# Splitting the last weight tile of a chunk's second product on VectorE, and one buffer for both parts of a split tile

## The chip, the cores and the metric

The kernel runs on one core of one Trainium2 chip. The metric is the device time of one launch in microseconds. Before the change three runs gave 2721.76, 2721.63 and 2718.28 us (median 2721.63 us). The execution that the profiler recorded took 2719.21 us, and its span is 2717.2 us.

## The reference

The reference is a trunk of two encoder layers, applied to 512 prompt tokens and 256 sample tokens with the same weights. The change lies in the loading of weights, and it alters arithmetic in the second half of a layer only: the feed-forward part with hidden width 4096 and model width 1024.

```python
def encoder_layer(x, l, ...):
...
    x = x + merged @ w_out
    h2 = rmsnorm(x, norm2_g)
    return x + jnp.square(jax.nn.relu(h2 @ w_ff1)) @ w_ff2
```

## The kernel before

All 768 tokens stand side by side on the free axis, and the model dimension lies on the 128 partitions, in 8 tiles. TensorE works on float32 data that is split in two: `hi` is the value rounded to the matmul's input type, `lo` is the rest. Each product of two split operands is three matmuls, `hi*hi`, `hi*lo` and `lo*hi`, which add up in PSUM (lines 1100 to 1103 for the second product). So every weight tile of 128x1024 is loaded, then split into `whi` and `wlo`, and TensorE reads both.

The feed-forward part goes through the hidden width in 8 chunks of 512. A chunk has a first product (`wf1`, lines 1017 to 1048) and a second product (`wf2`, lines 1081 to 1111). Both use a scheme of seven block products in place of eight. Its seven weight operands are made from four loaded blocks `a1`, `b1`, `b2`, `a2`: four are sums or differences (`P1` to `P4`, made on VectorE in line 250), three are the loaded blocks `a1`, `a2` and `b2` themselves. The order in which the first product takes them is `FW` (a1, P1, P2, a2, P3, P4, b2). The second product takes its seven products in the order `FP2` = (1, 2, 7, 6, 5, 3, 4), whose weight operands by `FW2` are a1, a2, P3, P2, P1, P4, b2. So **q=4, with weight operand b2, is the last product of a chunk**, and the first product of the next chunk begins with its own a1. Each q is 24 matmuls of 128x384. The last chunk of layer 1 uses the plain form (`wf2s`) for its second product. There are thus 15 chunks with seven-fold second products (7 in layer 1, 8 in layer 2) and 16 seven-fold first products.

The two kinds of weight operand are split in two ways (function `prefetch`). A sum or difference is split by `split`: ScalarE copies it to `whi` (line 210) and VectorE subtracts (`wlo = src - whi`, line 213). A loaded block (a1, a2, b2) is split by ScalarE and a DMA: ScalarE writes `whi` (line 294), then writes `-whi` into `wlo` (line 295), and a DMA that POOL issues adds the same block to `wlo` from DRAM (line 296):

```python
S.activation(hi, raw, AF.Copy)
S.activation(lo, raw, AF.Copy, scale=-1.0)
G.dma_start(out=lo, in_=acc, accum_op=ALU.add)
```

There are 93 of these accumulating DMAs. The second element that `ff_operand` returns is the DRAM address of the block, or None for a sum, and it decides which way `prefetch` takes.

Weights are prepared 8 plan entries ahead of their use (`AHEAD`), in a ring of four `whi` and four `wlo` buffers (`WB` = 4). A buffer comes free when TensorE has run the last matmul that reads it. The order of the instructions on each engine is settled at build time by a list scheduler with priorities; the additions of the second product from PSUM (line 1108, shown under its helper's line 1069) and the splits of the hidden activations (`h_split`, line 1065, shown under lines 210 and 213) have a raised priority. The activations' split for q=4 is `o2[4]`, made in line 1091.

Of the kernel before, what the change touches and what calls it, by code (L numbers as in the profile page):

```python
# [10 lines left out]
F32R = mybir.dt.float32r  # L11
# [5 lines left out]
P = 128  # L17
# [47 lines left out]
WB = 4  # L65
# [18 lines left out]
def trunk_kernel(ctx: ExitStack, tc: tile.TileContext, xT, wqk, wv, wx, wy, wg0, wg1, wa, wr, wo, wf1, wf2,  # L84
# [5 lines left out]
    wp = ctx.enter_context(tc.tile_pool(name="wp", bufs=1))  # L90
# [112 lines left out]
    def nm(s):  # L203
        uid[0] += 1
        return f"{s}_{uid[0]}"

    def split(hi, lo, src, eng="act"):

        if eng == "act":
            S.activation(hi, src, AF.Copy)  # L210
        else:
            V.tensor_copy(out=hi, in_=src)
        V.tensor_tensor(out=lo, in0=src, in1=hi.bitcast(F32), op=ALU.subtract)  # L213
# [29 lines left out]
    fw, fpool = {}, [None]  # L243

    def ff_operand(w, l, c, x):

        ep_, sub = fpool[0], w == "wf2"

        def two(out, u, v, op):
            V.tensor_tensor(out=fw[out], in0=fw[u], in1=fw[v], op=op)  # L250

        if x == "a1":
            for i, y in enumerate(("a1", "b1", "b2", "a2")):
                if i < 2:
                    fw[y] = ep_.tile([P, 1024], F32, tag="rw", name=nm("rw"), bufs=4)
                else:
                    fw[y] = wp.tile([P, 1024], F32, tag="raw", name=nm("raw"), bufs=3)
                fw["d" + y] = WT[w][l][c][i]
                nc.sync.dma_start(out=fw[y], in_=fw["d" + y])
            fw["P1"] = fw["P2"] = None  # L260
        if x in ("P1", "P2", "P3") and fw["P1"] is None:
            fw["P1"] = ep_.tile([P, 1024], F32, tag="ws", name=nm("ws"), bufs=2)
            two("P1", "b1", "b2", ALU.add)
        if x == "P2":
            fw[x] = ep_.tile([P, 1024], F32, tag="ws", name=nm("ws"), bufs=2)
            two(x, "P1", "a1", ALU.subtract if sub else ALU.add)
        elif x == "P3":
            fw[x] = fw["b1"]
            two(x, "a1", "b1", ALU.subtract if sub else ALU.add)
        elif x == "P4":  # L270
            fw[x] = fw["P2"]
            two(x, "a2", "P2", ALU.subtract if sub else ALU.add)
        return fw[x], fw.get("d" + x)

    def prefetch(upto):
        while len(ready) < min(upto, len(plan)):
            k = plan[len(ready)]
            acc = None
            if k[0] in ("wf1", "wf2"):
                (raw, acc), n = ff_operand(*k), 1024  # L280
            else:
                src = WT[k[0]]
                for x in k[1:]:
                    src = src[x]
                n = src.shape[1]
                raw = wp.tile([P, n], F32, tag="raw", name=nm("raw"), bufs=3)
                nc.sync.dma_start(out=raw, in_=src)
            hi = wp.tile([P, n], F32R, tag="whi", name=nm("whi"), bufs=WB)
            lo = wp.tile([P, n], F32R, tag="wlo", name=nm("wlo"), bufs=WB)
            if acc is None:  # L290
                split(hi, lo, raw)
            else:
# [4 lines that stand above are left out]
            ready.append((hi, lo))  # L297

    def wload(*key):
        i = pos[0]  # L300
        pos[0] += 1
        assert plan[i] == key, (plan[i], key)
        prefetch(i + 1 + AHEAD)
        r, ready[i] = ready[i], None
        return r
# [101 lines left out]
    def slot(tag, dt=F32):  # L407

        if (tag, dt) in spare:
            return spare.pop((tag, dt))  # L410
        t_ = slots(tag, dt)
        spare[tag, dt] = t_[:, 1]
        return t_[:, 0]
# [7 lines left out]
    def norm1(l, xt, alloc):  # L421

        nh = [slot(gh, F32R) for k in range(KT)]
        nl = [slot(gl, F32R) for k in range(KT)]
        ss, st_ = [], []

        def sums():
            if not st_:
                st_.append(slots(gx, F32R))
            return st_[0]  # L430

        for g in range(2):
            if g:
                prefetch(4)
            ss.append(squares(xt, g, alloc, sums, lambda k: prep(xt, vt[l][:, V_N1:V_N1 + KT], nh, nl, g, k)))
        return nh, nl, ss
# [6 lines left out]
    for k in range(KT):  # L443
        if k % 4 == 0:
            prefetch(1 + k // 4)
        nc.sync.dma_start(out=xt[k][:, 0:TA], in_=xT[k][:, 0:TA])
# [7 lines left out]
    for l in range(DEPTH):  # L454
# [292 lines left out]
        def chain():  # L747
            for kind, i in FILL:
                yield from (vproj(i, rtok) if kind == "wv" else proj(i, rtok) if kind == "wqk" else gate0(rb))

        n, it = 0, chain()
# [13 lines left out]
        for k in range(KT):  # L765
            af = ep.tile([P, T], F32, tag="af", name=nm("af"), bufs=4)
            G.dma_start(out=af, in_=ats[k])
            hi = ep.tile([P, T], F32R, tag="e", name=nm("ath"))
            lo = ep.tile([P, T], F32R, tag="e", name=nm("atl"))
# [6 lines left out]
        for j in range(KT):  # L776
# [3 lines left out]
            for g in range(2):  # L780
                off, n = GROUPS[g]
# [118 lines left out]
        def eslot(dt=F32):  # L900
            return ep.tile([P, T], dt, tag="e", name=nm("e"), bufs=16)

        def rslot(dt=F32):
            return recp.tile([P, T], dt, tag="r", name=nm("r"))

        rch, rcl = [], []
        for k in range(KT):
            hi, lo = eslot(F32R), eslot(F32R)
# [7 lines left out]
        for j in range(KT):  # L916
# [5 lines left out]
            for g in range(2):  # L922
                off, n = GROUPS[g]
# [4 lines left out]
            hi, lo = (rslot(F32R) if j < 4 else slot(gl, F32R) for i in range(2))  # L928
# [49 lines left out]
        for j in range(KT):  # L978
            w1 = wload("wo", l, j)
            for g in range(2):  # L980
                off, n = GROUPS[g]
# [21 lines left out]
        for c in range(NC_):  # L1003
# [13 lines left out]
            for i, (p, q) in enumerate(FP):  # L1017
                x, b = {1: ("a1", 2), 5: ("P1", 3), 6: ("P2", 2), 2: ("a2", 1), 7: ("P3", 2), 4: ("b2", 2), 3: ("P4", 3)}[q]
                if x not in ws:
                    ws[x] = [a.rearrange("p (h k c) -> p h k c", h=2, c=P) for a in wload("wf1", l, c, x)]  # L1020
                hi, lo = (a[:, p] for a in ws[x])
# [50 lines left out]
            if str2:  # L1072
# [8 lines left out]
                for q in FP2:  # L1081
# [10 lines left out]
                    hi, lo = (a.rearrange("p (r k c) -> p r k c", r=4, c=P) for a in wload("wf2", l, c, FW2[q]))  # L1092
# [19 lines left out]
            else:  # L1112
# [3 lines left out]
                for s in range(4):  # L1116
                    hi, lo = (a.rearrange("p (j k c) -> p j k c", j=2, c=P) for a in wload("wf2s", l, s))
# [99 lines left out]
```

## Time and profile before

| | us | share of the span |
|---|---|---|
| median of three runs | 2721.63 | |
| the profiled execution, own time | 2719.21 | |
| its span | 2717.2 | 100% |
| TensorE (PE) busy | 2617.4 | 96% |
| VectorE (DVE) busy | 1979.9 | 73% |
| ScalarE (ACT) busy | 1575.4 | 58% |
| POOL busy | 176.3 | 6% |

The seven-fold chunks of layer 1 run from about 870 to 1300 us, those of layer 2 from about 2223 us to the end. Matmuls overlap in the trace: one of 128x384 is shown as 0.33 us long, and the next starts 0.17 us after it. An idle time is counted from the shown end of the matmul before. In the rows, names that end in `wlo` and `whi` are weight parts, `raw`, `rw` and `ws` the unsplit weights, `sX`, `sY`, `sZ` and `e` activations, `d` a PSUM tile. The clock column of a stretch is the granted clock of TensorE as a share of 2.4 GHz; 0.50 is 1.2 GHz.

### The profile page before, as it was taken

How to read it: one execution, taken by the hardware profiler on the slowest of the kernel's cores; microseconds unless marked ns; L12 is line 12 of the kernel's file. 1: busy time of each engine (PE TensorE's matmuls, PEld its weight loads, DVE VectorE, ACT ScalarE, POOL GpSimd, SP SyncE). 2: the span in 40 equal slices, each digit the busy share in tenths (PEclk: the TensorE clock that was granted, in tenths of full speed). 3: DMA queues.
4: the chain of work that ended last, by engine and by line, in shares of the span. 5: the costliest groups of instructions: out<-in, count | busy, mean ns of one | idle time of the engine just before them, and what ended most of it. 6: DMA issues, size and time to landing. Idle time of an engine off the chain costs nothing. (4 is left out here: it accounts for less than half of the span.)

```text
span 2717.2 us, 40429 instructions
## 1 busy us (share of the span) xinstructions
PE 2617.4 (96%) x16096; PEld 2450.1 (90%) x16096; DVE 1979.9 (73%) x3243; ACT 1575.4 (58%) x2570; POOL 176.3 (6%) x227
## 2 busy tenths in 40 slices
PE   8999999999999999999999999999999999999999
PEld 8999888888889999998999998888888899999898
DVE  8878873797658777777678788637984587777776
ACT  7778871568336445444467878716683364544444
POOL 0000000000120000000100000000001100000000
PEclk9999999999999999999999999999999999999999
DMA  4111123112433444444421111231224334454543
GB/s 138 53 49 59 40 89 125 59 63 74 149 99 86 109 109 116 110 116 101 120 72 51 49 55 52 97 103 57 74 63 166 92 76 116 110 117 111 121 109 93
DMA packets 70876, 248.07 MB, mean 91 GB/s; under 512 B 8992, under 2 KB 12448, under 8 KB 70688
## 3 DMA queue, kind: packets, MB, share of 16 engines
q1 hardware_dynamic: 48384, 161.50, 18.7%
q0 software_dynamic: 21584, 83.37, 14.1%
q8 instruction: 126, 2.06, 0.3%
q10 hardware_dynamic: 720, 0.62, 0.1%
q14 instruction: 62, 0.51, 0.1%
HBM read 226.59 MB, written 18.87 MB: 90 GB/s over the span
## 5 line engine op out<-in xcount | busy, mean ns | idle before, releaser
L210 ACT ACTIVATE whi<-raw 128x1024 fp32r<-128x1024 f32 (+1 forms) x180 | 183.4, 1020 | 313.2 <-PE d L312 171.6
L213 DVE TENSOR_TENSOR wlo<-raw,whi 128x1024 fp32r<-128x1024 f32 (+1 forms) x180 | 215.1, 1199 | 33.1 <-ACT whi L210 32.0
L210 ACT ACTIVATE whi<-ws 128x1024 fp32r<-128x1024 f32 x93 | 98.5, 1059 | 158.3 <-DVE ws L250 61.5
L1103 PE MATMUL d<-sX,wlo 128*128 128x384 f32 x448 | 157.4, 351 | 27.8 <-DMA wlo<-wf 25.8
L1103 PE MATMUL d<-sZ,wlo 128*128 128x384 f32 x392 | 138.0, 352 | 26.5 <-DMA wlo<-wf 24.5
L1100 PE MATMUL d<-sX,whi 128*128 128x384 f32 x448 | 156.3, 349 | 4.2 <-DVE sZ L1069 4.1
L1102 PE MATMUL d<-sX,whi 128*128 128x384 f32 x448 | 155.1, 346 | 0.0
L312 PE MATMUL d<-sX,whi 128*128 128x512 f32 (+1 forms) x448 | 150.8, 337 | 0.5 <-DVE sX L213 0.5
L311 PE MATMUL d<-sZ,whi 128*128 128x512 f32 (+1 forms) x448 | 150.8, 337 | 0.3 <-DVE rec L403 0.3
L312 PE MATMUL d<-sZ,whi 128*128 128x512 f32 (+1 forms) x448 | 150.7, 336 | 0.0
L313 PE MATMUL d<-sZ,wlo 128*128 128x512 f32 (+1 forms) x448 | 150.6, 336 | 0.0
L296 POOL DMA_DIRECT2D wlo<-wf x93 | 81.5, 881 | 1031.3 <-ACT wlo L295 380.9
L294 ACT ACTIVATE whi<-raw 128x1024 fp32r<-128x1024 f32 x62 | 65.3, 1053 | 143.2 <-PE d L1102 119.9
L472 PE MATMUL d<-whi,sZ 128*128 128x256 f32 x512 | 147.5, 288 | 0.0
L472 PE MATMUL d<-whi,sY 128*128 128x256 f32 x512 | 147.4, 288 | 0.0
L201 ACT ACTIVATE p<-s,nb,sc 128x512 f32<-128x512 f32 (+1 forms) x192 | 134.6, 703 | 20.9 <-DVE nb L652 19.2
L474 PE MATMUL d<-whi,sX 128*128 128x256 f32 x512 | 144.8, 283 | 0.0
L474 PE MATMUL d<-whi,sZ 128*128 128x256 f32 x512 | 144.8, 283 | 0.0
L473 PE MATMUL d<-wlo,sY 128*128 128x256 f32 x512 | 144.7, 283 | 0.0
L473 PE MATMUL d<-wlo,sZ 128*128 128x256 f32 x512 | 144.7, 283 | 0.0
L213 DVE TENSOR_TENSOR wlo<-ws,whi 128x1024 fp32r<-128x1024 f32 x93 | 113.8, 1223 | 42.4 <-ACT whi L210 42.3
L1100 PE MATMUL d<-sZ,whi 128*128 128x384 f32 x392 | 137.0, 350 | 3.5 <-DVE sY L1069 3.5
(389 smaller groups left out, 9090.8 us busy)
## 6 DMA issues: line engine op xcount, KB each, us to landing
wlo<-wf POOLq DMA_DIRECT2D x93, 512.0 KB, 7.8
rw<-wf SPq DMA_DIRECT2D x62, 512.0 KB, 4.2
raw<-wf SPq DMA_DIRECT2D x62, 512.0 KB, 4.1
raw<-wqk SPq DMA_DIRECT2D x32, 512.0 KB, 3.9
raw<-wg SPq DMA_DIRECT2D x32, 512.0 KB, 3.8
raw<-wv SPq DMA_DIRECT2D x16, 512.0 KB, 3.8
raw<-wa SPq DMA_DIRECT2D x16, 512.0 KB, 3.8
raw<-wx SPq DMA_DIRECT2D x16, 512.0 KB, 3.7
```

What stands on the lines that cost most here:

```text
L201: return used(S.activation(*a, **k))
L210: S.activation(hi, src, AF.Copy)
L213: V.tensor_tensor(out=lo, in0=src, in1=hi.bitcast(F32), op=ALU.subtract)
L311: PE.matmul(ps, lhsT=wh, rhs=xh, start=(k == 0), stop=False)
L312: PE.matmul(ps, lhsT=wh, rhs=xl, start=False, stop=False)
L313: PE.matmul(ps, lhsT=wl, rhs=xh, start=False, stop=(k == n - 1))
L472: PE.matmul(j, lhsT=xh, rhs=hi[:, kk], start=(k == 0), stop=False)
L473: PE.matmul(j, lhsT=xh, rhs=lo[:, kk], start=False, stop=False)
L474: PE.matmul(j, lhsT=xl, rhs=hi[:, kk], start=False, stop=(k == 7))
L1100: PE.matmul(ps, lhsT=hi[:, r, k], rhs=oh[:, k], start=q in (1, 2, 7) and k == 0, stop=False, skip_group_check=True)
L1102: PE.matmul(ps, lhsT=hi[:, r, k], rhs=ol[:, k], start=False, stop=False, skip_group_check=True)
L1103: PE.matmul(ps, lhsT=lo[:, r, k], rhs=oh[:, k], start=False, stop=k == 1, skip_group_check=True)
```

## The change

```diff
@@ ff_operand
-        return fw[x], fw.get("d" + x)
+        return fw[x], None if sub and x == "b2" else fw.get("d" + x)
...
@@ prefetch
-            hi = wp.tile([P, n], F32R, tag="whi", name=nm("whi"), bufs=WB)
-            lo = wp.tile([P, n], F32R, tag="wlo", name=nm("wlo"), bufs=WB)
+            w_ = wp.tile([P, 2, n], F32R, tag="w", name=nm("w"), bufs=WB)
+            hi, lo = w_[:, 0], w_[:, 1]
```

For the second product (`sub` is true there) b2 now comes back without a DRAM address, so that `prefetch` splits it as it splits the sums: `whi` on ScalarE, `wlo` on VectorE. This takes out 15 of the 93 accumulating DMAs and the 15 `-whi` copies on ScalarE, and puts in 15 VectorE subtractions. All other blocks keep the DMA. Besides, the two parts of each split weight tile are now halves of one buffer, in a ring of four, where they were two buffers in two rings of four; the bytes are the same. Lines after 273 move down by one, so that line 1069 of before is line 1070 now. The order of TensorE's and SyncE's instructions is the same before and after, but for names. On VectorE and ScalarE it changes at these places.

VectorE, end of a second product in layer 2 (sixth chunk), before. `sX_25654` is the `lo` part of `o2[4]`; the rows of line 1069 add PSUM to the result (`d_25520` to `sZ_22019` and `d_25534` to `sZ_22021` are the two additions of q=3); `wlo_25517` is P1 of the next chunk.

```order
L213 TENSOR_TENSOR wlo_25369<-ws_25315,whi_25368 128x1024
L1069 TENSOR_TENSOR sZ_22022<-sZ_22022,d_25534 128x2x384
L213 TENSOR_TENSOR sX_25654<-e_25245,sX_25654 128x768
L250 TENSOR_TENSOR ws_25548<-ws_25514,rw_25440 128x1024
L1069 TENSOR_TENSOR sZ_22019<-sZ_22019,d_25520 128x2x384
L213 TENSOR_TENSOR wlo_25517<-ws_25514,whi_25516 128x1024
L1069 TENSOR_TENSOR sZ_22021<-sZ_22021,d_25534 128x2x384
L213 TENSOR_TENSOR wlo_25551<-ws_25548,whi_25550 128x1024
```

The same place in the changed kernel. `w_25040` is b2, `w_25133` is P1 of the next chunk, `sX_25267` is the `lo` part of `o2[4]`.

```order
L213 TENSOR_TENSOR w_24989<-ws_24938,w_24989 128x1024
L1070 TENSOR_TENSOR sZ_21730<-sZ_21730,d_25150 128x2x384
L213 TENSOR_TENSOR w_25040<-raw_24832,w_25040 128x1024
L1070 TENSOR_TENSOR sZ_21727<-sZ_21727,d_25136 128x2x384
L213 TENSOR_TENSOR w_25133<-ws_25131,w_25133 128x1024
L1070 TENSOR_TENSOR sZ_21729<-sZ_21729,d_25150 128x2x384
L213 TENSOR_TENSOR sX_25267<-e_24870,sX_25267 128x768
L250 TENSOR_TENSOR ws_25164<-ws_25131,rw_25058 128x1024
L250 TENSOR_TENSOR rw_25060<-rw_25058,rw_25060 128x1024
```

The new subtraction for b2 stands third. The `lo` part of `o2[4]` has moved from ahead of both additions of q=3 to behind them, and behind the split of the next chunk's P1. The same holds in the 14 chunks that are followed by another chunk; in the very last chunk the split of `o2[4]` stays ahead of the additions.

ScalarE at the same place, before. `whi_25420` and `wlo_25421` are b2, `whi_25448` and `wlo_25449` are a1 of the next chunk, `whi_25516` its P1.

```order
L210 ACTIVATE whi_25368<-ws_25315 128x1024
L294 ACTIVATE whi_25420<-raw_25206 128x1024
L294 ACTIVATE whi_25448<-rw_25440 128x1024
L295 ACTIVATE wlo_25421<-raw_25206 128x1024
L295 ACTIVATE wlo_25449<-rw_25440 128x1024
L210 ACTIVATE whi_25516<-ws_25514 128x1024
```

In the changed kernel:

```order
L210 ACTIVATE w_24989<-ws_24938 128x1024
L210 ACTIVATE w_25040<-raw_24832 128x1024
L295 ACTIVATE w_25066<-rw_25058 128x1024
L296 ACTIVATE w_25066<-rw_25058 128x1024
L210 ACTIVATE w_25133<-ws_25131 128x1024
L210 ACTIVATE w_25166<-ws_25164 128x1024
```

One copy is gone, and the `-whi` copy of the next a1 is one place nearer the front.

ScalarE in a first product, where its own b2 (`whi_25688`, `wlo_25689`) is split for the DMA, before; lines 1034 and 1036 evacuate PSUM.

```order
L1036 ACTIVATE e_25760<-d_25771 128x384
L294 ACTIVATE whi_25688<-raw_25444 128x1024
L1036 ACTIVATE e_25760<-d_25785 128x384
L295 ACTIVATE wlo_25689<-raw_25444 128x1024
L1011 ACTIVATE e_25759<-e_25759 128x384
```

In the changed kernel:

```order
L1037 ACTIVATE e_25370<-d_25380 128x384
L1037 ACTIVATE e_25370<-d_25394 128x384
L295 ACTIVATE w_25300<-raw_25062 128x1024
L296 ACTIVATE w_25300<-raw_25062 128x1024
L1012 ACTIVATE e_25369<-e_25369 128x384
```

The second evacuation now stands ahead of both copies.

## Rows read from the trace of the kernel before

**Rows 1.** Waits of PE: who waited for whom, total us, times, longest.
```profile
PE d L1103 <- DMA wlo<-wf: 50.2, 17, 4.1
...
PE d L1100 <- DVE sZ L1069: 4.1, 7, 0.6
PE d L1103 <- DVE wlo L213: 4.1, 14, 0.3
```

**Rows 2.** Timeline of PE, sixth chunk of layer 2: start, us, [idle before <-releaser].
```profile
2575.07 0.33 PE L1103 MATMUL d<-sX,wlo 128*128 128x384 f32 x1
2575.24 0.33 PE L1100 MATMUL d<-sX,whi 128*128 128x384 f32 x1
...
2579.35 0.69 PE L1103 MATMUL d<-sX,wlo 128*128 128x384 f32 x1 [3.60 <-DMA wlo<-wf]
```

**Rows 3.** Timeline of POOL at that place, and line 296 between 2571 and 2574 us.
```profile
2571.49 1.82 POOL L296 DMA_DIRECT2D wlo<-wf  x2 [25.99 <-DVE wlo L213]
...
DMA to landing us min/median/max: 7.8/8.6/9.3
```

**Rows 4.** Timeline of PE: waits for the DMA at other places.
```profile
870.45 0.44 PE L1103 MATMUL d<-sZ,wlo 128*128 128x384 f32 x1 [0.33 <-DMA wlo<-wf]
...
2223.05 0.44 PE L1103 MATMUL d<-sX,wlo 128*128 128x384 f32 x1 [0.30 <-DMA wlo<-wf]
...
2708.56 0.45 PE L1103 MATMUL d<-sX,wlo 128*128 128x384 f32 x1 [1.27 <-DMA wlo<-wf]
```

**Rows 5.** Stretches after a wait: us, busy by engine, PEclk, DMA share, GB/s.
```profile
900.50:907.50 7.00, 7.00 (x25) 7.00 (x26) 2.26 (x3) 0.29 (x1) 0.00 (x0) 0.57 0.11 21
...
2515.60:2522.60 7.00, 7.00 (x40) 7.00 (x41) 5.02 (x6) 2.50 (x3) 0.70 (x1) 1.00 0.49 124
...
2644.80:2651.80 7.00, 7.00 (x25) 7.00 (x26) 2.27 (x3) 0.30 (x1) 0.00 (x0) 0.58 0.10 20
```

**Rows 6.** Timeline of DVE, end of the sixth chunk of layer 2.
```profile
2570.03 1.22 DVE L213 TENSOR_TENSOR wlo<-ws,whi 128x1024 fp32r<-128x1024 f32 x1
2571.16 0.95 DVE L1069 TENSOR_TENSOR sZ<-sZ,d 128x768 f32<-128x768 f32 x1
2572.03 0.96 DVE L213 TENSOR_TENSOR sX<-e,sX 128x768 fp32r<-128x768 f32 x1
2572.90 1.22 DVE L250 TENSOR_TENSOR ws<-ws,rw 128x1024 f32<-128x1024 f32 x1
...
2576.03 0.95 DVE L1069 TENSOR_TENSOR sZ<-sZ,d 128x768 f32<-128x768 f32 x1
```

**Rows 7.** Timeline of ACT at the same place.
```profile
2568.25 1.04 ACT L294 ACTIVATE whi<-raw 128x1024 fp32r<-128x1024 f32 x1
...
2570.15 1.04 ACT L295 ACTIVATE wlo<-raw 128x1024 fp32r<-128x1024 f32 x1
2571.10 1.04 ACT L295 ACTIVATE wlo<-rw 128x1024 fp32r<-128x1024 f32 x1
```

**Rows 8.** Timeline of PE: two short waits; then stretches around them, columns as Rows 5.
```profile
276.09 0.41 PE L621 MATMUL t<-ident,qk 128*128 128x128 f32 x2 [1.76 <-DVE q L629]
...
1328.54 0.45 PE L311 MATMUL d<-e,whi 128*128 128x384 f32 x1 [1.22 <-ACT e L210]
...
276.00:280.00 4.00, 3.45 (x23) 2.96 (x24) 3.27 (x6) 3.33 (x7) 0.00 (x0) 1.00 0.00 0
...
1327.00:1333.00 6.00, 4.23 (x14) 3.65 (x14) 4.48 (x5) 2.92 (x5) 0.58 (x1) 0.73 0.52 175
```

**Rows 9.** Timeline of POOL in the first product; line 296 between 2540 and 2542 us.
```profile
2540.78 0.87 POOL L296 DMA_DIRECT2D wlo<-wf  x1 [5.14 <-ACT wlo L295]
...
DMA to landing us min/median/max: 7.8/7.8/7.8
```

**Rows 10.** Timelines of ACT and PE in the first product, around its b2.
```profile
2533.04 0.47 ACT L1036 ACTIVATE e<-d 128x384 f32<-128x384 f32 x1
...
2542.75 0.42 PE L1030 MATMUL d<-e,wlo 128*128 128x384 f32 x1
```

## Prediction

> **What bounds the kernel now.** I read the page's busy shares first (TensorE is busy nearly all the span, so only its idle time and its clock can be won back), then the waits of TensorE, then the timelines of all engines at the largest wait, and last the granted clock behind each wait.
>
> In the waits, one line stands out: the third matmul form of the second product waits for the accumulating DMA, 50.2 us in 17 times [rows 1]. The timeline places them. Two of the 17 are the first tiles of a layer's first chunk, 0.33 and 0.30 us [rows 4]. The other 15 are one in each seven-fold second product, always at the third matmul of q=4, the first that reads `wlo` of b2: in the sixth chunk of layer 2, q=4 starts at 2575.24 us, runs two matmuls and then stands until 2579.35, idle 3.60 us [rows 2]. The reader is to see the late transfer there: POOL issues it at 2571.49 and it lands 7.8 us later, at 2579.3 [rows 3]. It cannot be issued sooner because its `-whi` copy on ScalarE runs only from 2570.15 to 2571.19 [rows 7]. The 15 waits hold 50.2 - 0.63 = 49.6 us; 1.27 of it is the very last chunk's [rows 4], so 48.3 us fall on the other 14.
>
> A second loss hangs on the same wait. Matmuls start every 0.17 us [rows 2], 40 in an undisturbed 7 us; behind most of these waits only 25 to 32 run in 7 us [rows 5], since the granted clock has dropped for a while to the lower of its two levels, 1.2 GHz. Taking the 7 us behind each of the 14 waits, the clock column reads 0.57, 1.00, 0.77, 0.60, 0.76, 0.76, 0.76, 0.58, 0.76, 0.76, 0.57, 1.00, 0.78, 0.58 (first, one of the two untouched, and last in [rows 5]). The shortfalls from 1 add up to 3.75, so 7 x 3.75 = 26.2 us of full-speed work are lost; over the 12 that fell this is 2.2 us each.
>
> **The change, part by part.**
>
> *b2's DMA goes.* With it go the 15 waits, 49.6 us, and the clock loss behind them, 26.2 us: 75.8 us at most.
>
> *b2's subtraction comes, on VectorE.* It is of the kind at 2570.03, 1.22 us [rows 6], 15 x 1.22 = 18.3 us of VectorE work. Its `whi` is ready at 2569.3 [rows 7], and its place is behind the addition that starts at 2571.16, so it runs from about 2572.0 to 2573.2. TensorE wants it at 2575.6. By itself it is hidden, with 2.4 us in hand.
>
> *What it pushes back.* The `lo` part of `o2[4]`, also an operand of q=4 (from its second matmul), ran at 2572.03 [rows 6], more than 2 us early. In the new order it stands behind both additions of q=3. The second of these reads PSUM that q=3's last matmul writes; that one starts at 2575.07 and ends at 2575.40 [rows 2]. So: b2's split to 2573.2; q=3's first addition and the split of the next P1 (0.87 and 1.14 us from start to start) to 2575.4; the second addition from 2575.45, 0.87 us to the next start; the split of `o2[4]` 0.96 us, to 2577.3. TensorE's second matmul of q=4 then starts at 2577.3, where 2575.41 was free. Idle, counted as the profile does from the first matmul's shown end at 2575.57: **1.7 us**. This wait follows from the program's order and not from a transfer, so it should be alike in 14 chunks: 14 x 1.7 = 24 us. The very last chunk keeps the old order and has none. From below, the wait cannot be less than one addition and one split after q=3's end, 1.7 us; from above, each us by which the next P1's split were late would be added.
>
> *The clock behind the new wait.* No row shows a wait of exactly this kind. The nearest are eight waits of 1.2 to 1.8 us. Seven, such as 1.76 us at 276.09, leave the clock at 1.00; one, 1.22 us at 1328.54 with another right behind, brings the stretch to 0.73 [rows 8]. So the bounds are nothing and 14 x 2.2 = 31 us. I take one in eight, 4 us.
>
> *Next chunk's a1.* It keeps its DMA and is needed sooner now. Its `-whi` copy moves from 2571.10 to 2570.15 [rows 7], so its issue moves to the 2571.49 that b2's had. With 7.8 us it lands at 2579.3; the pair's slower one, 9.3 us, would give 2580.8 [rows 3]. TensorE resumes at 2577.3, has 23 matmuls of q=4 left (4.0 us), and wants a1's `lo` at 2581.6. Covered; if the cover failed by x us, it would cost 14x.
>
> *The first product's b2.* Its DMA already lands when it is wanted: the matmul at 2542.75 is stretched to 0.42 us [rows 10]. There a PSUM evacuation of 0.47 us now goes ahead of both copies. Part of it was between the copies before, so the `-whi` copy is later by between 0 and 0.47 us; I take 0.1, 16 times: 1.6 us.
>
> *SP's queue.* b2's unsplit buffer is released by VectorE's subtraction at 2573.2, where ScalarE's copy released it at 2571.2, so the load that takes it over starts 2 us later. It holds a block whose first use, a weight sum on VectorE, comes after q=4 in the order. I take 0.
>
> *One buffer for both parts.* `whi`'s half now comes free with the last `lo` matmul, 0.17 us later than before. Weights are prepared several tiles ahead, so I take 0. The few VectorE and ScalarE rows swapped elsewhere I take as 0, within 2 us either way.
>
> *The sum.* 49.6 + 26.2 - 24 - 4 - 1.6 = 46 us off. The profiled execution's own time is 2719.2, which gives 2673. The three runs lie 1.35 us above it on average (the median 2.4), so the forecast is **2674 us**.
>
> **The rivals.**
>
> *A. The clock falls behind every new wait.* For it: 12 of the 14 waits of the old kind did so. Against it: the seven short waits that did not. Cost 31 in place of 4: 2674 + 27 = 2701; with most but not all falling, 2690 to 2701.
>
> *B. VectorE gets through sooner.* The list before shows two small waits per chunk on VectorE, 0.6 at the third product and 0.29 at the sixth [rows 1]; if these shrink (4.1 us for 7 of the one, an estimated 3.5 for the other layer's 6, and 4.1 for 14 of the other), with no clock loss, the time is 2674 - 12 - 4 - 1.6 = 2656. Against it: VectorE's order up to there is the same. If the 1.7 us were not there either, it would be some 2632, but the order excludes that unless the activations' split is not wanted where I think.
>
> *C. Slower: the DMA of the next a1 is starved and TensorE waits there.* Mechanism: POOL issues at 2571.49, in the middle of an unbroken run of VectorE work, which now ends with the split of `o2[4]` and two weight sums (1.14 us each from start to start, [rows 6]) at about 2579.6. If the transfer really began only then, it would land at 2587.4, 5.8 us after it is wanted: 14 x 5.8 = 81 us, and 2674 + 81 = 2755. It decides from a landing 46 / 14 = 3.3 us late, 2584.9, that is 13.4 us after issue. Against it: b2's DMA was issued inside just such a run and took 7.8 us [rows 3], and one issued while VectorE paused took 7.8 us as well [rows 9]. The Trainium skill, page "SBUF — State Buffer", section "Who interferes with whom", says that a VectorE instruction with two SBUF inputs contends with GpSimd instructions that read SBUF. The same section adds that DMAs issued from GpSimd can be starved of descriptors. By a broad reading of it, the time would be C's; the two equal landings speak against that reading here.
>
> *D. The change does not do it.* Excluded for the DMA: the order holds 15 fewer issues on POOL.
>
> **How the numbers follow.** Forecast 0.68, A 0.16, B 0.09, C 0.04, and 0.03 for a gain that is eaten by something unseen. The forecast's own range is 2667 to 2684 (half of A's clock price upward; the small terms downward). The range of 8 in 10 takes in A and B's smaller form: 2656 to 2701. A measurement of this kernel can tell about 0.2%, 5 us, from no change; the forecast, A and B are all faster by far more: 0.94. Within 0.2%: 0.02. Slower: 0.04.
>
> **What would show it.** Right: the waits of TensorE on `wlo<-wf` fall from 17 to a few tenths of a us each, but for one tile in the first product; a new line, the second product's second matmul form waiting for VectorE's split (line 213), 14 times near 1.7 us; 78 accumulating DMAs; the granted clock at 1.00 behind most of the new waits. Wrong: a DMA wait of us at the next chunk's a1 (C); clock shares near 0.6 to 0.8 behind the new waits (A); no new wait (B); or waits well over 2 us there, which would say that the split of the next P1 is late too.

## The result and the profile after

The changed kernel's median is **2673.0 us** (three runs, 2672.29 to 2674.40), against 2721.63 before: a ratio of 0.9828, 95% interval 0.9815 to 0.9841. The forecast was 2674.0 with a range of 2656 to 2701. The profiled execution took 2674.40 us with a span of 2672.6, so against the 2719.21 and 2717.2 of before it is 44.8 us shorter; the sum of the prediction was 46.

From the page, busy time (share of the span) and instructions:

```profile
PE 2597.6 (97%) x16096; PEld 2431.5 (91%) x16096; DVE 2000.1 (75%) x3258; ACT 1561.8 (58%) x2555; POOL 163.1 (6%) x212
```

VectorE has 20.2 us more than the 1979.9 of before, in 15 more instructions. Now the waits of TensorE (who waited for whom: us in total, times, longest). Lines 1101, 1103 and 1104 are the first, second and third matmul form of the second product, each one higher than before; both parts of a weight are now called `w`.

```profile
PE d L1103 <- DVE sZ L213: 12.2, 7, 1.7
PE d L1103 <- DVE sX L213: 12.2, 7, 1.7
...
PE d L1101 <- DVE sZ L1070: 4.8, 8, 0.6
PE d L1104 <- DVE w L213: 4.1, 14, 0.3
PE d L1101 <- DVE sY L1070: 3.8, 6, 0.6
...
PE d L1104 <- DMA w<-wf: 0.4, 1, 0.4
PE d L1031 <- DMA w<-wf: 0.3, 2, 0.2
```

The 50.2 us in 17 times of [rows 1] are 0.4 us in one, at the first tile of layer 1's first chunk; the 15 waits for b2 are gone. Line 1031 is the third form of the first product. New are the first two lines: 14 waits that hold 24.4 us, all on VectorE's line 213, the subtraction that makes a `lo` part. The 0.3 us waits at P4 are as before (4.1 us), and those for the additions of line 1070 went from 4.1 and 3.5 us to 4.8 and 3.8. In the timeline of TensorE, sixth chunk of layer 2, the new wait stands at the second matmul of q=4, where [rows 2] has the third matmul of q=4 waiting 3.60 us:

```profile
2538.42 0.33 PE L1104 MATMUL d<-sX,w 128*128 128x384 f32 x1
2538.60 0.34 PE L1101 MATMUL d<-sX,w 128*128 128x384 f32 x1
2540.67 0.44 PE L1103 MATMUL d<-sX,w 128*128 128x384 f32 x1 [1.74 <-DVE sX L213]
```

The timeline of VectorE at that place, beside [rows 6], tells why:

```profile
2535.37 1.22 DVE L213 TENSOR_TENSOR w<-raw,w 128x1024 fp32r<-128x1024 f32 x1
2536.71 0.95 DVE L1070 TENSOR_TENSOR sZ<-sZ,d 128x768 f32<-128x768 f32 x1
2537.59 1.22 DVE L213 TENSOR_TENSOR w<-ws,w 128x1024 fp32r<-128x1024 f32 x1
2538.79 0.95 DVE L1070 TENSOR_TENSOR sZ<-sZ,d 128x768 f32<-128x768 f32 x1
2539.66 0.95 DVE L213 TENSOR_TENSOR sX<-e,sX 128x768 fp32r<-128x768 f32 x1
2540.53 1.22 DVE L250 TENSOR_TENSOR ws<-ws,rw 128x1024 f32<-128x1024 f32 x1
```

From the top: b2's new subtraction, q=3's first addition, the split of the next chunk's P1, q=3's second addition, and only then the `lo` part of `o2[4]`, from 2539.66 to 2540.61. TensorE starts again at 2540.67. The second addition needs q=3's last matmul (2538.42 to 2538.75 above), so it cannot be earlier than 2538.8, and one addition plus one split stand between that matmul and TensorE's next. The chain that ended last runs along VectorE (start, us, what):

```profile
2536.71 0.95 DVE sZ L1070
2537.67 1.14 DVE w L213
...
2539.66 0.96 DVE sX L213
2540.63 0.04 issue
2540.67 0.44 PE d L1103
```

It comes to the second addition by the split of P1, which ends at 2538.81, only 0.06 us behind q=3's last matmul. So both hold the addition back equally long, and an earlier split of P1 alone would hardly have shortened this wait.

Next, the granted clock in the 7 us behind a new wait, columns as in [rows 5]. In this execution 12 of the 14 stretches stand at 1.00, like the middle row; the other two are shown around it, each with 31 matmuls where 40 fit.

```profile
960.80:967.80 7.00, 7.00 (x31) 7.00 (x32) 5.41 (x6) 2.12 (x3) 0.00 (x0) 0.76 0.28 99
2540.70:2547.70 7.00, 7.00 (x40) 7.00 (x41) 6.98 (x7) 3.57 (x4) 0.36 (x1) 1.00 0.29 92
2602.70:2609.70 7.00, 6.98 (x31) 6.98 (x32) 5.42 (x6) 2.11 (x3) 0.00 (x0) 0.76 0.05 19
```

Where the time came from is seen at the second product's second matmul form in each layer: instructions, duration in ns, and the starts of the first and the last. Before:

```profile
L1102 PE MATMUL d<-sZ,whi x392: 333/334/525, 869.8 to 1296.6; 128*128 128x384 f32 x196
...
L1102 PE MATMUL d<-sX,whi x448: 333/334/522, 2222.4 to 2712.2; 128*128 128x384 f32 x150
```

After:

```profile
L1103 PE MATMUL d<-sZ,w x392: 333/334/522, 870.4 to 1275.9; 128*128 128x384 f32 x196
...
L1103 PE MATMUL d<-sX,w x448: 333/334/522, 2201.9 to 2667.6; 128*128 128x384 f32 x150
```

The stretch of layer 1 shrank from 426.8 to 405.5 us and that of layer 2 from 489.8 to 465.7, together 45.4. Up to the first and between the two, where some rows of VectorE and ScalarE have traded places too, 0.8 us were added. So the whole difference arises in the seven-fold chunks. Of the 45.4, DMA waits gave 49.8 and the new waits took 24.4, a balance of 25.4, which leaves 20.0. The clock behind the waits gave 26.2 - 3.4 = 22.8, so small terms took 2.8. Of these, 1.0 us is the growth of the waits for line 1070, and 0.3 the waits of line 1031; the rest is not placed.

Last, the DMA of the next chunk's a1, in the timeline of ScalarE, that of POOL, and line 297 between 2530 and 2540 us:

```profile
2533.49 1.04 ACT L296 ACTIVATE w<-rw 128x1024 fp32r<-128x1024 f32 x1
```

```profile
2534.83 0.88 POOL L297 DMA_DIRECT2D w<-wf  x1 [26.24 <-DVE w L213]
```

```profile
DMA to landing us min/median/max: 5.7/5.7/5.7
```

It is issued inside VectorE's run, which has a pause of 0.12 us and no other until a1 has landed at 2540.5, while TensorE is still at work on q=4. Over all 78 issues of the line, none took longer than 8.9 us:

```profile
DMA to landing us min/median/max: 5.4/7.3/8.9
```

### The profile page after: what moved, and what is told of

It reads as the page before. It is cut to its first block, busy times and chain, and to the rows that moved or that the text cites. A ratio compares the mean times of both kernels' runs of the same rounds, so it can differ in the third digit from the quotient of the medians.

```text
span 2672.6 us, 40396 instructions
## 1 busy us (share of the span) xinstructions
PE 2597.6 (97%) x16096; PEld 2431.5 (91%) x16096; DVE 2000.1 (75%) x3258; ACT 1561.8 (58%) x2555; POOL 163.1 (6%) x212
## 4 chain that ended last, share of the span: by engine, by line
PE 68%; DVE 18%; ACT 8%; issue 5%; DMA 1%; ACTq 0%; DVEq 0%; POOLq 0%
PE d L314 6%; PE d L313 6%; PE d L312 6%; PE d L1031 5%; PE d L1029 5%; PE d L1030 5%; DVE w L213 4%; PE d L474 4%; PE d L475 4%; PE d L473 4%; PE s L650 3%; PE d L1104 2%; PE d L1103 2%; PE d L1101 2%; PE d L337 2%
## 5 line engine op out<-in xcount | busy, mean ns | idle before, releaser
L210 ACT ACTIVATE w<-raw 128x1024 fp32r<-128x1024 f32 (+1 forms) x195 | 199.0, 1022 | 324.9 <-PE d L314 163.0
L213 DVE TENSOR_TENSOR w<-raw,w 128x1024 fp32r<-128x1024 f32 (+1 forms) x195 | 234.0, 1204 | 38.4 <-ACT w L210 37.3
L1103 PE MATMUL d<-sX,w 128*128 128x384 f32 x448 | 151.3, 338 | 12.2 <-DVE sX L213 12.2
L1101 PE MATMUL d<-sX,w 128*128 128x384 f32 x448 | 151.8, 339 | 4.8 <-DVE sZ L1070 4.8
L1104 PE MATMUL d<-sX,w 128*128 128x384 f32 x448 | 151.6, 338 | 2.1 <-DVE w L213 2.0
L312 PE MATMUL d<-sZ,w 128*128 128x512 f32 (+1 forms) x448 | 150.8, 337 | 0.5 <-DVE rec L404 0.5
L313 PE MATMUL d<-sZ,w 128*128 128x512 f32 (+1 forms) x448 | 150.8, 337 | 0.0
L313 PE MATMUL d<-sX,w 128*128 128x512 f32 (+1 forms) x448 | 150.7, 336 | 0.0
L314 PE MATMUL d<-sZ,w 128*128 128x512 f32 (+1 forms) x448 | 150.6, 336 | 0.0
L473 PE MATMUL d<-w,sZ 128*128 128x256 f32 x512 | 148.0, 289 | 0.0
L473 PE MATMUL d<-w,sY 128*128 128x256 f32 x512 | 147.9, 289 | 0.0
L201 ACT ACTIVATE p<-s,nb,sc 128x512 f32<-128x512 f32 (+1 forms) x192 | 134.5, 702 | 21.7 <-DVE nb L653 20.2
L475 PE MATMUL d<-w,sX 128*128 128x256 f32 x512 | 145.3, 284 | 0.0
L475 PE MATMUL d<-w,sZ 128*128 128x256 f32 x512 | 145.3, 284 | 0.0
L474 PE MATMUL d<-w,sY 128*128 128x256 f32 x512 | 145.2, 284 | 0.0
L474 PE MATMUL d<-w,sZ 128*128 128x256 f32 x512 | 145.2, 284 | 0.0
L1103 PE MATMUL d<-sZ,w 128*128 128x384 f32 x392 | 132.5, 338 | 12.2 <-DVE sZ L213 12.2
L1101 PE MATMUL d<-sZ,w 128*128 128x384 f32 x392 | 133.0, 339 | 3.8 <-DVE sY L1070 3.8
L1104 PE MATMUL d<-sZ,w 128*128 128x384 f32 x392 | 132.8, 339 | 2.4 <-DVE w L213 2.1
L312 PE MATMUL d<-sY,w 128*128 128x512 f32 (+1 forms) x384 | 129.3, 337 | 0.5 <-DVE rec L404 0.5
```

What stands on the lines that cost most here:

```text
L201: return used(S.activation(*a, **k))
L312: PE.matmul(ps, lhsT=wh, rhs=xh, start=(k == 0), stop=False)
L313: PE.matmul(ps, lhsT=wh, rhs=xl, start=False, stop=False)
L314: PE.matmul(ps, lhsT=wl, rhs=xh, start=False, stop=(k == n - 1))
L473: PE.matmul(j, lhsT=xh, rhs=hi[:, kk], start=(k == 0), stop=False)
L474: PE.matmul(j, lhsT=xh, rhs=lo[:, kk], start=False, stop=False)
```

## The experiments

The theory going in: the gain is the late DMA of b2 and the clock behind it; what is left, 1.74 us in 14 chunks, is an order on VectorE in which `o2[4]` stands behind q=3's additions; the joined buffer does nothing. Rivals: the joined buffer carries part of the gain; VectorE is full, so that taking the 1.74 us away at one place brings them back at another.

**1. Each half of the change alone.** First the split with buffers apart, an edit of the kernel before:

```diff
-        return fw[x], fw.get("d" + x)
+        return fw[x], None if sub and x == "b2" else fw.get("d" + x)
```

> The VectorE split of b2 alone, with the two rings of four buffers as before. Theory (the gain comes from b2's DMA leaving the path, the common buffer is worth nothing beside it): 2672 us, within 3 of the changed kernel, the same 14 waits of 1.74 us on the activations' split. Rival (the common buffer carries part of the gain): 2680 or more.

Measured: 2668.97 us (2666.29 to 2673.21), ratio 0.9813 (0.9796 to 0.9830). The same 14 waits of 1.74 us are there, and the time is at the lower edge of what was expected. The split alone gives the whole gain.

Then the joined buffer alone, b2 again by DMA, an edit of the changed kernel:

```diff
-        return fw[x], None if sub and x == "b2" else fw.get("d" + x)
+        return fw[x], fw.get("d" + x)
```

> The common buffer alone; b2 of the second product keeps its accumulating DMA. In this build ScalarE's order also changes: b2's -whi copy now comes straight behind its whi copy, one copy (0.95 us) sooner, so that the DMA is issued sooner. Theory (the wait is the DMA's lateness, so it shrinks by just the 0.95 us of earlier issue): 14 waits of 1.3 to 3.1 us, 13 us less, and a part of the 26 us of clock loss back, 2690 to 2708 us in all. Rival (the buffer and its order do nothing): 2719 to 2723 us, waits as before.

Measured: 2703.49 us (2694.65 to 2706.24), ratio 0.9933 (0.9910 to 0.9955), so alone it is worth some 18 us, by the interval 12 to 24. Its waits of TensorE, and the timelines of ScalarE, POOL and TensorE at the sixth chunk of layer 2:

```profile
PE d L1104 <- DMA w<-wf: 39.0, 16, 3.7
```

```profile
2492.65 1.04 ACT L295 ACTIVATE w<-raw 128x1024 fp32r<-128x1024 f32 x1
2493.59 1.04 ACT L296 ACTIVATE w<-raw 128x1024 fp32r<-128x1024 f32 x1
2494.54 1.04 ACT L295 ACTIVATE w<-rw 128x1024 fp32r<-128x1024 f32 x1
```

```profile
2495.08 0.88 POOL L297 DMA_DIRECT2D w<-wf  x1 [25.45 <-PE d L1104]
```

```profile
2502.71 0.44 PE L1104 MATMUL d<-sX,w 128*128 128x384 f32 x1 [2.56 <-DMA w<-wf]
```

b2's `-whi` copy now follows its `whi` copy directly; before, a1's `whi` copy ran between them [rows 7]. The DMA is issued 2.43 us after the start of the `whi` copy, where it was 3.24 [rows 3, 7], and the waits shrink from 50.2 to 39.0 us, 11.2 where 13 were expected; those at q=4 last 1.19 to 3.67 us. The seven-microsecond stretches behind them lose 21.4 us to the clock, where the prediction counted 26.2 before. That is 16 of the 18. So joining the buffers has an effect, but by way of the order of ScalarE's copies around a DMA that the split then takes out.

**2. Joined and apart, side by side.** The profiled execution of the split alone was 8 us shorter than that of the changed kernel, which had run on its own, so both were run again side by side on one chip, with no further edit.

> The changed kernel once more, beside the next one, so that joined buffers and buffers apart stand on one chip: 2671 to 2675.

> b2's split on VectorE with buffers apart, once more, beside the changed kernel. If the joined buffer costs a few us: 3 to 5 us below it. If it costs nothing and the difference of the earlier calls was the clock of single executions or the chip: within 2 us of it.

Measured: joined 2669.64 us (2667.51 to 2672.20), 1.4 below the range expected, ratio 0.9819 (0.9804 to 0.9833); apart 2670.09 (2667.18 to 2670.87), ratio 0.9818 (0.9803 to 0.9833). There is no difference that these runs can tell. Beside the split the joined buffer costs nothing that can be measured; the 8 us were one profiled execution against another.

**3. Where `o2[4]` stands in VectorE's order.** The priority offset of the two instructions that split `o2[4]`, `URGE // 3` in the changed kernel, was raised to its full value:

```diff
-                        with tc.high_priority(offset=URGE // 3):
+                        with tc.high_priority(offset=URGE):
```

> The changed kernel with the raised priority of the activations' split for q=4 put up to that of the other raised work (300 instead of 100). In VectorE's order it then stands ahead of the weight splits of P1 and P4. Theory (VectorE has no slack in this stretch, so who goes first only moves the wait): the 14 waits at q=4 vanish, and waits at the third matmul of q=5 (0.4 us) and of q=3 (about 2 us, 0.29 now) take their place: 2673 to 2682 us. Rival (VectorE has slack and only the order was bad): 2645 us.

What is called the theory there is the rival "VectorE is full" of above. Measured: 2674.92 us (2674.62 to 2675.06), ratio 0.9834 (0.9817 to 0.9850). The wait at q=4 is gone, and one of equal size has come at q=3. Waits of TensorE, and its timeline there:

```profile
PE d L1104 <- DVE w L213: 29.7, 29, 1.8
```

```profile
2530.07 0.44 PE L1104 MATMUL d<-sX,w 128*128 128x384 f32 x1 [0.27 <-DVE w L213]
...
2536.36 0.44 PE L1104 MATMUL d<-sX,w 128*128 128x384 f32 x1 [1.83 <-DVE w L213]
```

Now it is P4's `lo` split that comes too late, 14 times 1.83 us. By this run alone, the rival "VectorE is full" could stand. Then the offset in between:

```diff
-                        with tc.high_priority(offset=URGE // 3):
+                        with tc.high_priority(offset=URGE // 2):
```

> The changed kernel with that priority at 150. The split of the activations for q=4 then takes the place of the next chunk's P1 sum, which is not wanted before that chunk's third block and goes behind the additions of q=3. Theory (the 1.74 us wait is the price of an order in which work for the next chunk stands ahead of work for q=4): all 14 waits gone, 24.4 us, with the 3.4 us of clock loss behind two of them; P4's wait of 0.29 stays or shrinks: 2645 us (2640 to 2650). Rival (VectorE is too full for any order): another wait of 1 to 2 us shows up, 2660 us or more.

Measured: 2638.87 us (2637.40 to 2640.46), ratio 0.9701 (0.9686 to 0.9716), below what was expected. In its waits nothing is left of line 213 in the second product; these two lead there:

```profile
PE d L1101 <- DVE sZ L1070: 4.4, 7, 0.6
PE d L1101 <- DVE sY L1070: 4.1, 7, 0.6
```

VectorE's timeline, same chunk:

```profile
2503.13 0.95 DVE L213 TENSOR_TENSOR sX<-e,sX 128x768 fp32r<-128x768 f32 x1
2504.00 0.95 DVE L1070 TENSOR_TENSOR sZ<-sZ,d 128x768 f32<-128x768 f32 x1
2504.86 1.22 DVE L213 TENSOR_TENSOR w<-ws,w 128x1024 fp32r<-128x1024 f32 x1
2506.00 0.94 DVE L1070 TENSOR_TENSOR sZ<-sZ,d 128x768 f32<-128x768 f32 x1
2506.86 1.22 DVE L213 TENSOR_TENSOR w<-raw,w 128x1024 fp32r<-128x1024 f32 x1
```

TensorE there, second and third matmul of q=3:

```profile
2505.79 0.34 PE L1103 MATMUL d<-sX,w 128*128 128x384 f32 x1
2506.13 0.44 PE L1104 MATMUL d<-sX,w 128*128 128x384 f32 x1
```

`o2[4]` is split at 2503.13, ahead of P4's `lo` at 2504.86 and b2's at 2506.86, and no wait of TensorE for any of the three is left in the list. P4's is only just in time: it ends at 2506.08, and the matmul that reads it starts at 2506.13, 0.17 us behind the pace. The same work, 1998.5 us of VectorE against 2000.1, now costs TensorE no such wait: it was the order, and the rival falls. Gone are the 14 waits (24.4 us), P4's 14 (4.1) and the two clock drops (3.4), together 31.9 of the 34 us between this median and the changed kernel's 2673.0. The two were not run side by side. With buffers apart, on another chip:

> b2 split on VectorE, the split of o2[4] with the middle priority offset as in the fourth run, and the two parts in buffers of their own as before the change. If joining the buffers costs a few us beside the split (the run with buffers apart had a median of 2669.0 where the changed kernel had 2673.0, in different calls), this comes out at 2631 to 2636, below the fourth run's 2638.9. If the joined buffer costs nothing and those 4 us were the clock (3.4 us of it fell in the profile of the changed kernel and none here), it stands within 2 us of 2638.9.

Measured: 2634.28 us (2633.50 to 2635.33), ratio 0.9689 (0.9674 to 0.9703). That is the time that was expected if joining costs a few us. But the intervals of the two ratios overlap, and these two kernels were not run side by side, so it stays open whether joining costs something at this offset.

**4. More of the splits on VectorE.** On top of the middle offset, the first product's b2 too, and beside it the middle offset once more on the same chip:

```diff
-        return fw[x], None if sub and x == "b2" else fw.get("d" + x)
+        return fw[x], None if x == "b2" else fw.get("d" + x)
```

> The fourth run (joined buffers, o2[4] at the middle offset), with b2 of the first product split on VectorE too: 16 more subtractions of 1.22 us there, 16 DMAs less on POOL. TensorE's waits for the accumulating DMA are only tenths of a us by now, so a theory that counts DMA waits expects 0 to 2 us less than 2638.9. A rival that has VectorE as the next engine to run late expects waits of TensorE on line 213 in the first product and 2 to 12 us more.

> The fourth run again (joined buffers, o2[4] at the middle offset), beside the next: if the 4 us between it and the runs of buffers apart, and with both b2 on VectorE, were the chip of that call, it comes out at 2634 to 2636 here, with a ratio near 0.9695; if they were the kernels, at 2638 to 2640.

> The same with the first product's b2 on VectorE too, again. By the count of waits at most 1 us below the run before it; by the earlier calls' medians 4 us below it.

Measured: both b2 2634.54 us (2633.80 to 2635.30), ratio 0.9690 (0.9674 to 0.9706), 4 us below the first run of the middle offset, where at most 2 were expected. Then, side by side, the middle offset alone 2636.68 (2635.89 to 2638.33), ratio 0.9705 (0.9691 to 0.9720), between the two times that were expected, and both b2 2633.54 (2633.42 to 2634.79), ratio 0.9694 (0.9679 to 0.9708). The runs of these two do not overlap, and the 3 us are more than the 1 us by the count of waits, but they are under the 0.2% that was taken as the limit. Where they come from is not shown. The two profiled executions of the middle offset hold two and three falls of the clock outside the seven-fold chunks while TensorE was at work, some 1.7 us each, and those of both b2 none. There is no new wait on line 213, so the rival of a late VectorE falls.

Then a2 of both products, and at last every weight tile, so that no accumulating DMA of these products is left:

```diff
-        return fw[x], None if x == "b2" else fw.get("d" + x)
+        return fw[x], None if x in ("b2", "a2") else fw.get("d" + x)
```

> Split on VectorE besides b2 also a2, in both products: some 31 more subtractions of 1.22 us, 38 us of VectorE work. VectorE is busy 2018 of 2632 us with both b2. If its share counts, there is room and the time stays within 3 us of 2634.5. If its order in the second product counts, where its work runs unbroken from the third tile to the last, each of the 15 chunks can lose up to one subtraction: 5 to 20 us slower, as waits of TensorE on lines 213 or 1070 in the second product.

```diff
-        return fw[x], None if x == "b2" else fw.get("d" + x)
+        return fw[x], None
```

> All weight tiles of both products split on VectorE, no accumulating DMA left: against the run before it a1 too, some 31 more subtractions, 38 us more of VectorE work. By VectorE's share (about 2094 of 2640 us) no change; by its order in the second product 10 to 50 us slower than 2634.5, with the granted clock below 1.00 there.

Measured: 2634.70 us (2633.06 to 2635.47), ratio 0.9696 (0.9682 to 0.9711), and 2633.60 (2632.79 to 2635.17), ratio 0.9694 (0.9677 to 0.9710). From the page of the last one, busy time (share of the span) and instructions:

```profile
PE 2585.6 (98%) x16096; PEld 2427.3 (92%) x16096; DVE 2083.5 (79%) x3336; ACT 1491.5 (57%) x2477; POOL 94.4 (4%) x134
```

Of the two outcomes that were set out for these runs, the loss of 5 to 50 us by VectorE's order did not come, and the one by its share held: 78 more subtractions than in the middle-offset kernel, some 85 us of VectorE work, find room with no new wait of TensorE. A transfer that nobody waits for costs nothing here that can be measured, and taking it away gains at most those 3 us.

All versions from the middle offset on beat both kernels, with ratios to before of 0.969 to 0.971 where the change has 0.982 to 0.983. The smallest step to them from the changed kernel is one number, the offset.

## Why the prediction was right

- **The removed waits.** Predicted 49.6 us off, the 15 waits for b2, and all 15 are gone. With what the first tiles of the layers gave, it is 49.8: 50.2 [rows 1] against 0.4.
- **The new wait.** Predicted 1.7 us in 14 chunks, 24 us, from the order of VectorE's instructions alone; measured 1.74 in 14, 24.4, none in the last chunk. The third experiment shows the cause: the split's place in the order, moved, takes the wait with it. That the P1 split and q=3's last matmul end together, as the prediction's sum has it (2575.4 for both), is seen in the chain above.
- **The clock.** One in eight falls, 4 us, was the choice between 0 and 31. Two of 14 fell, by 0.24 each: 7 x 0.48 = 3.4 us. That it came so near is luck. With the same 14 waits the clock fell twice in another execution of the changed kernel, not at all in the two of the split alone, and four times behind the 14 waits of 1.83 us in experiment 3. The eight waits that the share was taken from do not settle it either. The one at 276.09 us left the clock at 1.00 in the kernel before [rows 8]; in the changed kernel it is as long, and the same stretch behind it stands at 0.57:

```profile
275.80 0.41 PE L622 MATMUL t<-ident,qk 128*128 128x128 f32 x2 [1.77 <-DVE q L630]
...
276.00:280.00 4.00, 4.00 (x19) 3.72 (x18) 2.02 (x4) 3.60 (x8) 0.00 (x0) 0.57 0.00 0
```

- **The sum.** With the 26.2 won back, the 4 of above and the 1.6 of the first product, the prediction had 20.6 us of clock and small terms, and the stretches leave 20.0. The parts lie a little further off: the clock gave 22.8 where 22.2 was forecast, the small terms took 2.8 where 1.6 was.
- **The first product's b2.** Predicted 1.6 us. The matmuls there wait for DMAs 0.3 us in all. The weight loads of the same line wait 2.4 us in 8 times, and this is no more than 1.2 us above the 1.2 in 4 times of before, so the term is at most 1.5. Before:

```profile
PEld d L1030 <- DMA wlo<-wf: 1.2, 4, 0.4
```

After:

```profile
PEld d L1031 <- DMA w<-wf: 2.4, 8, 0.5
```

- **One buffer.** Taken as 0 beside the split, and it is (runs side by side, 0.45 us apart). The reason given, that a part comes free 0.17 us later, was only half of what it does: without the split it also reorders ScalarE's copies, which was worth some 18 us. The prediction did not look at this, and its 0 is right because the split takes that DMA out.
- **The rivals.** A (the clock falls behind every wait): 12 of 14 stayed at 1.00. B (VectorE sooner): its time did not come, since P4's waits stayed 4.1 us and those at the third product did not shrink either; the middle offset shows what P4's and the new wait were worth. C (a1's DMA starved): it decided from a landing 13.4 us after issue, and the longest of all 78 landings is 8.9, the one in the chunk shown 5.7. The Trainium skill, page "SBUF — State Buffer", section "Who interferes with whom", says that DMAs issued from GpSimd can be starved of descriptors. It also reports that `tensor_tensor` was not seen to stall a DMA. `tensor_tensor` is all that VectorE ran around that transfer, so the trace agrees with the latter by its 5.7 us; the broad reading in the prediction left this out. D: no b2 DMA of the second product was left.

## What to carry over

When a late transfer is removed by giving its work to an engine, read what then stands ahead of the next operand in that engine's order: here a VectorE that was idle a quarter of the time still caused 14 waits, and one number, which moves the priority of one pair of instructions, took them away. Price the wait that is left by the instructions between the last input and the waiting matmul; that gave 1.7 us before any run. Two halves of a change need not add up: 18 and 51 us alone were 48 together, because both acted on the same transfer.

## What the runs showed that was not expected

Of three offsets for `o2[4]` the one in the middle is best. They gave 2673, 2638.9 and 2674.9 us; the two ends lose about the same time at different tiles. Offsets between these three were not tried.

Behind longer idles of TensorE the granted clock fell more often, though not strictly. In the changed kernel, the split alone, their repeats and the run with the full offset there are 70 waits of 1.74 or 1.83 us at q=4 or q=3; behind 8 of them the 7 us stood at 0.76, behind the others at 1.00. All 8 are in kernels with one buffer, but the mean clock of all executions, 0.997 to 1.000 joined and 0.997 to 0.999 apart, shows no such difference. Behind 24 of the 26 waits of 2.17 us and more that the kernel before and the buffer alone show at q=4 it fell, and behind all 15 of 3.0 us and more. The same kernel with the same 14 waits had two drops in each of two executions, at different chunks. Two waits of 1.76 us elsewhere, the one at 276.09 of [rows 8] and its like in layer 2, are as long in all 14 profiled executions, and the clock fell behind 11 of these 28. Why one such wait drops the clock and the next does not stays open.
